# A two-layer hybrid diffusion step on one core: weight splits earlier, residual tiles in token halves, modulation rows moved

## The chip, the cores and the metric

One core of a Trainium2 chip runs the whole program in one launch. The metric is the device time of an execution in microseconds; the median of several runs is compared.

## What is computed

Two layers of a diffusion backbone over T = 640 tokens (128 of context, 512 latent ones), width 1024, all in float32. Each layer (from the reference, cut):

```python
mod = silu(cond) @ p['w_mod'][l] + p['b_mod'][l]
sh_a, sc_a, g_a, sh_f, sc_f, g_f = jnp.split(mod[:, None, :], 6, axis=-1)
xn = rmsnorm(h, p['norm_mix'][l]) * (1 + sc_a) + sh_a
proj = xn @ p['w_in'][l]
# three branches read proj: latent attention, gated linear attention, gated DeltaNet
y = jnp.sum(gates * proj_b, axis=2) @ p['w_out'][l]
h = h + g_a * y
xf = rmsnorm(h, p['norm_ffn'][l]) * (1 + sc_f) + sh_f
gu = xf @ p['ffn_w_in'][l]
h = h + g_f * ((silu(gu[..., :D_FF]) * gu[..., D_FF:]) @ p['ffn_w_out'][l])
```

A last rmsnorm gives the output, beside the caches and states of the branches. `cond` is one vector for the context tokens and one for the latent ones, so each row of `mod` has two columns.

## The kernel before

Activations stand channel by token: eight tiles of 128 channels by 640 tokens for h, and tokens are taken in two halves c = 0, 1 of HF = 320. Every float32 operand of a matmul is split in a high and a low part (xh, xl; wh, wl), and a product is three matmuls of 128x320: xh·wh, xl·wh, xh·wl. A weight block is 128 by up to 512, that is up to four k-steps of 128; an output tile with eight k-steps (wo, fg, fu, misc, mq) is 24 matmuls in each half, 48 in all.

Class `Stream` (L286) holds all such work of a layer as a list of units, one for a weight block or one product. `plain` (L312) adds one, `product` (L316) one of the seven block products of a gated pair, `step` (L341) issues one k-step, `to` runs until a tile is done, `fill` puts steps beside other work. `ahead` (L333) loads blocks and splits them: `wsplit` (L488) casts wr to wh on ACT (L493) and subtracts wl = wr - wh on POOL or DVE (L494). The ring of split blocks has three buffers. Accumulators are `gm` (three in PSUM). L539 (`mm_k`) is the matmul of plain units, L531 (`mm_block`) that of block products. A scheduler of the language then reorders the instructions of each engine by priority, keeping what depends on what; the order on an engine is fixed when the program is built.

A layer runs: norm and modulation (`modulate`, L677), input projections and the three branches, output tiles wo0 to wo7, the second norm (`modulate_in`, L696, and `token_sums`, L710, which makes the sums xeh, xel of token halves that block products need), then the FFN. Its 22 gate and up tile pairs (fg, fu) come in three groups of 8, 7 and 7. The first two pairs are plain tiles, the other 20 are seven block products of 12 matmuls each. A pair ends in th = silu(gate)·up, cast to ah (L1911) with al = th - ah (L1912). After each group its share of the second FFN matmul follows: tiles fo0_0 to fo0_7, then fo1, fo2, eight tiles each (42 or 48 matmuls); `h_update` (L725) adds gate times tile to h.

After wo7 and after fo2_7 comes a joint. `resid_posts` (L731) updates h tile by tile and `Norm.add` squares it (ACT, L659) and adds it to nacc (DVE, L660). The last tile is treated by halves (`Norm.end`). `Norm.fin` (L666) sums over partitions with a matmul by ones into `cs` (L669) and takes the reciprocal root as exp(-ln/2) on ACT (L551, L553), each with a table load in front. `join` (L746) orders this: half 0, then half 1, with the modulation of a half after its root. The tiles that follow (fg0 and fu0, or misc and mq0 of layer 1) need all eight modulated tiles, and no matmul that is left over stands beside that.

`ModVe` (L588) makes the rows of `mod` on DVE: one product with accumulation (L614) for each 128x512 piece of w_mod and each of the two conditions. They are called at chosen places (`some(...)`): beside wo tiles, in `close` of a pair, and in `fo_post` after a fo tile, and keep their order.

Of the kernel before, what the change touches and what calls it, by code (L numbers as in the profile page):

```python
# [18 lines left out]
P = 128  # L19
# [12 lines left out]
NPL = 2  # L32

# [254 lines left out]
class Stream:  # L288
# [44 lines left out]
    def ahead(self):  # L333
        u = self.units[self.u]
        i, c = u["i"], u["c"]
        self._split(i)
        top = max(self.w)
        for j in range(1, 3):
            self._load(top + j)
        if len(self.w) < self.ring and (top == i or (c == 1 and u["prod"] is None)):  # L340
            self._split(top + 1)  # L341

    def step(self):
# [14 lines left out]
        if self.k == kn:  # L358
# [5 lines left out]
            if u["prod"]:  # L364
# [36 lines left out]
def tile_hybrid(ctx: ExitStack, tc, a):  # L401
# [247 lines left out]
    class Norm:  # L649
        def __init__(self):  # L650
            self.acc = sp.tile([P, T], F32, name="nacc", tag="nacc", bufs=1)
            self.ps = self.last = None
# [8 lines left out]

        def end(self, h, c):
# [68 lines left out]
    def resid_posts(names, hs, g, nm, keep=False):  # L731
        def post(ps, c=None, d=0):
            if d < 7:
                h_update(hs, d, ps, g)
                nm.add(d, hs[d])
                if keep:
                    dma(hsp[d], hs[d])
            else:
                h_update(hs, d, ps, g, (c,))
                nm.end(hs[d], c)  # L740
                if keep:
                    dma(hsp[d][:, HS[c]], hs[d][:, HS[c]])
        for d in range(8):
            G.posts[names[d]] = lambda ps, c=None, d=d: post(ps, c, d)

    def join(name, hs, nm, after, pre=None):  # L746

        if pre:
            pre()
        G.to(name + "/0")  # L750
        G.steps(5)
        nm.fin(0)
        G.to(name)
        after(0, range(4))
        nm.fin(1)
        after(0, range(4, 8))
# [789 lines left out]

    for l in range(L):
# [485 lines left out]
```

## Time and profile before

| | |
|---|---|
| median of 3 runs | 2968.56 us (2960.3, 2970.24, 2968.56) |
| the profiled execution | 2961.4 us |
| its span, first to last instruction | 2959.3 us |
| mean granted clock of TensorE in it | 0.963 |
| busy: PE, DVE, ACT, POOL | 2691.0, 1888.7, 1390.0, 988.0 us |

The profiled execution is 7.2 us below the median and 2.1 above its own span. PE is TensorE, DVE VectorE, ACT ScalarE, POOL GpSimd. In a row, `a<-b,c` names what is written and read, L the line of the kernel; an idle time is that of the engine just before the instruction, with what ended it. A clock of 1.00 is 2.4 GHz, 0.50 is 1.2 GHz.

### The profile page before, as it was taken

To read this page: it belongs to the slowest core of one execution; us is meant where nothing else is said; L and a number is where in the kernel's file an instruction comes from. 1 tells how busy PE (TensorE), PEld (TensorE's weight loads), DVE (VectorE), ACT (ScalarE), POOL (GpSimd) and SP (SyncE) were. 2 spreads that over 40 slices of the span, in tenths; PEclk is the share of its full clock that TensorE was granted. 3 is DMA by queue.
4 is the path that set the end of the run, shared out by engine and by line. 5 is a ranking of instruction groups with operands and counts; after the bars stand their busy time and mean duration, and the time that the engine had idled before them with its cause. 6 is when DMAs were issued, how large, how long until landed. Compare 5 with 4: busy or idle time off the path is not lost. (4 is left out here: it accounts for less than half of the span.)

```text
span 2959.3 us, 50253 instructions
## 1 busy us (share of the span) xinstructions
PE 2691.0 (91%) x18964; PEld 2439.6 (82%) x18964; DVE 1888.7 (64%) x3712; ACT 1390.0 (47%) x2624; POOL 988.0 (33%) x748
## 2 busy tenths in 40 slices
PE   6899998899999789999988899988999997899998
PEld 4788887788879679898978888876878796899997
DVE  4766575657647687777458576566566466847374
ACT  5574646533333643434466555654333335424244
POOL 3443232333326313232335323233433352232313
PEclk9999999999999899999999999998999998999999
DMA  5254433255424234332223533332645151322222
GB/s 202 88 167 132 97 85 84 90 154 157 137 75 160 68 100 139 98 119 85 89 79 113 178 89 90 76 99 69 185 138 157 41 176 60 100 82 78 76 68 76
DMA packets 303601, 322.37 MB, mean 109 GB/s; under 512 B 164832, under 2 KB 175904, under 8 KB 303360
## 3 DMA queue, kind: packets, MB, share of 16 engines
q1 hardware_dynamic: 303360, 319.16, 36.4%
q8 instruction: 150, 2.46, 0.3%
q14 instruction: 91, 0.75, 0.1%
HBM read 271.25 MB, written 47.82 MB: 108 GB/s over the span
## 5 line engine op out<-in xcount | busy, mean ns | idle before, releaser
L494 POOL TENSOR_TENSOR wl<-wr,wh 128x512 fp32r<-128x512 f32 x496 | 691.7, 1398 | 1609.1 <-ACT wh L493 1371.5
L539 PE MATMUL gm<-xh,wh 128*128 128x320 f32 x2176 | 554.3, 330 | 39.1 <-ACT wh L493 11.5
L539 PE MATMUL gm<-xh,wl 128*128 128x320 f32 x2176 | 545.0, 323 | 19.9 <-POOL wl L494 19.9
L539 PE MATMUL gm<-xl,wh 128*128 128x320 f32 x2176 | 543.2, 323 | 11.3 <-DVE xl L707 3.8
L493 ACT ACTIVATE wh<-wr 128x512 fp32r<-128x512 f32 x496 | 305.5, 620 | 490.0 <-PE gm L539 231.5
L539 PEld LDWEIGHTS gm<-xh,wh 128*128 128x128 f32 x2176 | 378.5, 196 | 62.9 <-ACT wh L493 13.3
L539 PEld LDWEIGHTS gm<-xh,wl 128*128 128x128 f32 x2176 | 380.5, 195 | 32.2 <-POOL wl L494 23.7
L539 PEld LDWEIGHTS gm<-xl,wh 128*128 128x128 f32 x2176 | 381.5, 195 | 30.2 <-DVE xl L693 8.1
L614 DVE CUSTOM_DVE_ANT_0 ctb<-wmt,cbb 128x512 f32<-128x512 f32 x320 | 288.2, 901 | 2.8
L531 PE MATMUL gm<-xh,wh 128*128 128x320 f32 x640 | 203.9, 319 | 29.5 <-ACT wh L493 21.9
L531 PE MATMUL gm<-xh,wl 128*128 128x320 f32 x640 | 198.9, 311 | 3.3 <-POOL wl L494 3.3
L531 PE MATMUL gm<-xl,wh 128*128 128x320 f32 x640 | 198.8, 311 | 0.0
L493 ACT ACTIVATE wh<-ws 128x512 fp32r<-128x512 f32 x160 | 101.0, 632 | 175.9 <-PE gm L531 154.5
L531 PE MATMUL gm<-xeh,wh 128*128 128x320 f32 x480 | 152.8, 318 | 17.6 <-DVE su L1945 10.0
L539 PE MATMUL gm<-ah,wh 128*128 128x320 f32 x704 | 163.8, 310 | 3.9 <-ACT wh L493 3.7
L539 PE MATMUL gm<-al,wh 128*128 128x320 f32 x704 | 163.4, 308 | 0.0
L539 PE MATMUL gm<-ah,wl 128*128 128x320 f32 x704 | 162.5, 308 | 0.0
L531 PEld LDWEIGHTS gm<-xh,wh 128*128 128x128 f32 x640 | 121.4, 190 | 41.4 <-ACT wh L493 30.8
L1053 ACT ACTIVATE VN<-ch 64x64 f32<-64x64 f32 x320 | 70.0, 219 | 181.8 <-DVE vs L1050 160.3
L728 DVE SCALAR_TENSOR_TENSOR h<-gm,mod,h 128x128 f32<-128x128 f32 (+2 forms) x192 | 73.2, 432 | 118.8 <-PE gm L539 118.5
L531 PE MATMUL gm<-xel,wh 128*128 128x320 f32 x480 | 148.9, 310 | 0.0
L531 PE MATMUL gm<-xeh,wl 128*128 128x320 f32 x480 | 148.9, 310 | 0.0
(787 smaller groups left out, 5507.6 us busy)
## 6 DMA issues: line engine op xcount, KB each, us to landing
wr<-in_wall_dram SPq DMA_DIRECT2D x352, 256.0 KB, 2.7
wmt<-in_wmodt_dram SPq DMA_DIRECT2D x160, 256.0 KB, 3.0
wq<-in_wall_dram SPq DMA_DIRECT2D x80, 256.0 KB, 2.6
wr<-in_wfo_dram SPq DMA_DIRECT2D x64, 256.0 KB, 2.7
wr<-in_wbr_dram SPq DMA_DIRECT2D x48, 256.0 KB, 2.6
wm<-in_wmod_dram SPq DMA_DIRECT2D x16, 512.0 KB, 8.6
cbb<-in_condb_dram SPq DMA_DIRECT2D x14, 512.0 KB, 4.8
wr<-in_wfo_dram SPq DMA_DIRECT2D x32, 192.0 KB, 2.4
```

The costliest lines, as they stand in the source:

```text
L493: se.activation(wh[:, :w], wr[:, :w], AF.Copy)
L494: (ve if lo == "dve" else ge).tensor_tensor(wl[:, :w], wr[:, :w], wh[:, :w], op=ALU.subtract)
L531: pe.matmul(ps, w_[:, wsl], x_[k], start=(start and i == 0), stop=(stop and i == 2), skip_group_check=True)
L539: pe.matmul(ps[:, c, :HF], w_[:, wsl], x_[kx][:, c * HF:(c + 1) * HF], start=(start and i == 0), stop=(stop and i == 2))
L614: ins = ve.tensor_tensor_reduce(self.t, wm, self.c[:, i], 0.5, 0.0, ALU.mult, ALU.add, accum_out=acc[h][:, m - m0, i:i + 1])
L728: ve.scalar_tensor_tensor(hs[d][:, s:e], ps[:, c, s - c * HF:e - c * HF], g[:, d, i:i + 1], hs[d][:, s:e], op0=ALU.mult, op1=ALU.add)
L1053: se.activation(VN[d * 64:(d + 1) * 64, h, n], ps[h * 64:(h + 1) * 64, 1], AF.Copy)
```

## The change

1. `ahead` wants the blocks up to i + 2 split for products and half units, i + 1 for whole ones; before it was one ahead, with conditions.
2. The last three tiles of each residual sum (wo5 to wo7, fo2_5 to fo2_7) run by token halves: all three for half 0, then all three for half 1 (`by_halves`). Each half loads and splits its weights anew and has its own accumulator. The tiles that follow (fg0, fu0; misc, mq0 of layer 1) run by halves too. `Norm.part` squares a half; `Norm.fin` has an accumulator of its own. `join` runs one step of the second halves, the sum of half 0, then modulation tiles and steps in turn. The prescaling of us or h (`prescale`) goes by tile.
3. Rows 16 to 23 of layer 1's modulation are made in layer 0's FFN instead of the DeltaNet chain of layer 1. They are all called beside fo tiles, six products for a tile instead of three, and none in `close` for layer 1's rows. Beside wo: five products for each of wo0 to wo4 instead of four for wo0 to wo6.
4. al = th - ah runs on POOL instead of DVE.

```diff
@@ Stream
-        top = max(self.w)
         for j in range(1, 3):
-            self._load(top + j)
-        if len(self.w) < self.ring and (top == i or (c == 1 and u["prod"] is None)):
-            self._split(top + 1)
+            self._load(max(self.w) + j)
+        want = i + (1 if c is None else 2)
+        while len(self.w) < self.ring and max(self.w) < want and max(self.w) + 1 < len(self.subs):
+            self._split(max(self.w) + 1)
...
+            elif last and u["own"]:
+                with self.prio("pp"):
+                    self.posts.pop(name)(self.ps.pop(name)[:, :, :HF])
+                self.done.add(name)
@@ Norm, join
+        def part(self, h, c):
+            sq = tmp()
+            se.activation(sq[:, HS[c]], h[:, HS[c]], AF.Square)
+            ve.tensor_tensor(self.acc[:, HS[c]], self.acc[:, HS[c]], sq[:, HS[c]], op=ALU.add)
...
         def fin(self, c):
-            self.ps = psg("cs") if self.ps is None else self.ps
+            ps = psb([P, HF], "cs")
...
+    def join(name, l, nm, after):
+
+        G.to(f"{name}7.{l}:0")
+        G.steps(1)
         nm.fin(0)
-        G.to(name)
-        after(0, range(4))
+        for i in range(4):
+            after(0, range(2 * i, 2 * i + 2))
+            G.steps(2)
+        G.to(f"{name}7.{l}:1")
+        G.steps(1)
         nm.fin(1)
-        after(0, range(4, 8))
         after(1, range(8))
@@ the list of units
+    def by_halves(jobs, own):
+
+        for c in range(2):
+            for name, src, kt, xs in jobs:
+                for k0 in range(0, kt, 4):
+                    kn = min(4, kt - k0)
+                    G.plain(f"{name}:{c}" if own else name, src[:, k0 * P:(k0 + kn) * P], k0, kn, xs, c, k0 + kn == kt, False,
+                            own=own, key=f"{name}:{c}")
...
-            k8("misc", "in")
-            k8("mq0")
+            by_halves([w8("misc"), w8("mq0")], False)
...
-        for d in range(8):
-            k8(f"wo{d}", "post" if d == 7 else None)
+        for d in range(8 - NHV):
+            k8(f"wo{d}")
+        by_halves([w8(f"wo{d}") for d in range(8 - NHV, 8)], True)
...
-                k8(f"fg{f}", "in" if f == 0 else None)
-                k8(f"fu{f}", pre=lead and (lambda q=lead: q.fetch("A21", "A22")))
+                if f == 0:
+                    by_halves([w8("fg0"), w8("fu0")], False)
...
+            if tail:
+                by_halves([(f"fo{gi}_{d}.{l}", a["wfo"][l, d, :, f0 * P:f1 * P], f1 - f0, ("a",)) for d in range(8 - NHV, 8)], True)
@@ modulation rows and al
-                    mst = ModVe(bd, 4, 2).steps(l, range(16, 16 + OPT["mc"]))
+                    mst = ModVe(bd, 4, 2).steps(l, range(16 if l == 0 else NXT, 16 + OPT["mc"]))
...
-            nxt = mv.steps(l + 1, range(16), True) if l + 1 < L else iter(())
+            nxt = mv.steps(l + 1, range(NXT), True) if l + 1 < L else iter(())
...
-                ve.tensor_tensor(al[:, f - f0], th, ah[:, f - f0], op=ALU.subtract)
+                ge.tensor_tensor(al[:, f - f0], th, ah[:, f - f0], op=ALU.subtract)
...
-                elif f1 < NF:
-                    some(nxt, 2)
...
-                    some(nxt, 3 if (gi, d) != (gl_ - 1, 7) else 1000)
+                    some(nxt, 6)
```

Three places in the built order (NHV is 3, NXT is 24, a name with a number is one buffer).

**First place**: ACT at the start of the FFN of layer 0, before. L715 shifts us, L722 casts the token sums, wh_10324 is the weight block that L539 waits for.

```order
L722 ACTIVATE xeh_10048<-tsum_10238 128x960 [waits DVE_49]
L715 ACTIVATE us7_10061<-us7_10061,mod0_102 128x128
L722 ACTIVATE xeh_10048<-tsum_10249 128x960 [waits DVE_49]
L715 ACTIVATE us7_10061<-us7_10061,mod0_102 128x512 [waits Activation_49]
L493 ACTIVATE wh_10324<-wr_10279 128x512 [waits DMAHW3_49,PE_49]
L493 ACTIVATE wh_10370<-wr_10310 128x512 [waits DMAHW4_49,PE_49]
L1905 ACTIVATE th_10340<-gm_10281 128x640 [waits PE_49]
L722 ACTIVATE xeh_10048<-tsum_10260 128x960 [waits DVE_49]
```

The same place in the change: L727 and L734 are the lines of the shifts and casts now, and wh_10386 is the second block of fg0 in half 1.

```order
L734 ACTIVATE xeh_9926<-tsum_10286 128x960 [waits DVE_49]
L727 ACTIVATE us6_9544<-us6_9544,mod0_102 128x128
L727 ACTIVATE us6_9544<-us6_9544,mod0_102 128x512 [waits Activation_49]
L727 ACTIVATE us3_9541<-us3_9541,mod0_102 128x128
L727 ACTIVATE us3_9541<-us3_9541,mod0_102 128x512
L734 ACTIVATE xeh_9926<-tsum_10297 128x960 [waits DVE_49]
L727 ACTIVATE us7_9545<-us7_9545,mod0_102 128x128
L734 ACTIVATE xeh_9926<-tsum_10308 128x960 [waits DVE_49]
L727 ACTIVATE us7_9545<-us7_9545,mod0_102 128x512 [waits Activation_49]
L500 ACTIVATE wh_10386<-wr_10365 128x512 [waits DMAHW3_49,PE_49]
L500 ACTIVATE wh_10404<-wr_10384 128x512 [waits DMAHW4_49,PE_49]
L500 ACTIVATE wh_10422<-wr_10402 128x512 [waits DMAHW5_49,PE_49,Pool_49]
```

The cast of the weight block stands behind the shifts and casts of the token sums in both; in the change it is the block of fg0's second half, and two more blocks stand next to it.

**Second place**: PE at the end of wo7 of layer 0, before. gm_10082 is wo7, cs the sum over partitions for both halves.

```order
L669 MATMUL cs_10138<-th_10115,ones_79 128x320 [waits Activation_49]
L539 MATMUL gm_10082<-xh_98,wh_10078 128x320
L539 MATMUL gm_10082<-xl_99,wh_10078 128x320
L539 MATMUL gm_10082<-xh_98,wl_10079 128x320
L539 MATMUL gm_10082<-xh_98,wh_10078 128x320
L539 MATMUL gm_10082<-xl_99,wh_10078 128x320
L539 MATMUL gm_10082<-xh_98,wl_10079 128x320
L539 MATMUL gm_10082<-xh_98,wh_10078 128x320
L539 MATMUL gm_10082<-xl_99,wh_10078 128x320
L539 MATMUL gm_10082<-xh_98,wl_10079 128x320
L669 MATMUL cs_10138<-nacc_9530,ones_79 128x320 [waits Activation_49]
L669 MATMUL cs_10138<-th_10115,ones_79 128x320 [waits Activation_49]
```

In the change, gm_10080 is the second half of wo5, and cs_10084 the sum for half 0 alone.

```order
L546 MATMUL gm_10080<-xh_98,wh_10035 128x320 [waits DVE_49,Activation_49]
L546 MATMUL gm_10080<-xl_99,wh_10035 128x320
L546 MATMUL gm_10080<-xh_98,wl_10036 128x320 [waits Pool_49]
L681 MATMUL cs_10084<-nacc_9531,ones_79 128x320 [waits DVE_49]
L546 MATMUL gm_10080<-xh_98,wh_10035 128x320
L546 MATMUL gm_10080<-xl_99,wh_10035 128x320
L546 MATMUL gm_10080<-xh_98,wl_10036 128x320
L546 MATMUL gm_10080<-xh_98,wh_10035 128x320
L546 MATMUL gm_10080<-xl_99,wh_10035 128x320
L546 MATMUL gm_10080<-xh_98,wl_10036 128x320
L546 MATMUL gm_10080<-xh_98,wh_10035 128x320
L681 MATMUL cs_10084<-th_10072,ones_79 128x320 [waits Activation_49]
```

The sum of half 0 stood among the matmuls of wo7's second half, next to that of half 1; now it stands at the head of the second half of wo5, with nearly three half tiles of matmuls behind it.

**Third place**: DVE in a pair of group 0 of layer 0, before. ISA is a modulation product (L614), su (L1945) a sum that the next block product's accumulator waits for.

```order
L1953 TENSOR_TENSOR th<-th,su 128x320
L1912 TENSOR_TENSOR al<-th,ah 128x640
L614 ISA ctb,mod_102<-wmt,cbb 128x512
L614 ISA mod_102 128x1
L494 TENSOR_TENSOR wl<-wq,wh 128x512
L614 ISA ctb,mod_102<-wmt,cbb 128x512
L614 ISA mod_102 128x1
L614 ISA ctb,mod_102<-wmt,cbb 128x512
L614 ISA mod_102 128x1
L1945 TENSOR_TENSOR su<-gm,sn 128x320
L614 ISA ctb,mod_102<-wmt,cbb 128x512
L614 ISA mod_102 128x1
```

In the change (L621, L1983; the subtraction that makes al is on POOL):

```order
L1991 TENSOR_TENSOR th<-th,su 128x320
L621 ISA ctb,mod_102<-wmt,cbb 128x512
L621 ISA mod_102 128x1
L621 ISA ctb,mod_102<-wmt,cbb 128x512
L621 ISA mod_102 128x1
L621 ISA ctb,mod_102<-wmt,cbb 128x512
L621 ISA mod_102 128x1
L501 TENSOR_TENSOR wl<-wq,wh 128x512
L621 ISA ctb,mod_102<-wmt,cbb 128x512
L621 ISA mod_102 128x1
L1983 TENSOR_TENSOR su<-gm,sn 128x320
```

al is gone from this engine; three products stand in a row ahead of wl, and su stands behind all four instead of three.

## Rows read from the trace of the kernel before

**Rows 1.** The page, parts 1 and 2: PE, and the clock by slices.
```profile
PE 2691.0 (91%) x18964; PEld 2439.6 (82%) x18964; DVE 1888.7 (64%) x3712; ACT 1390.0 (47%) x2624; POOL 988.0 (33%) x748
PEclk9999999999999899999999999998999998999999
```

**Rows 2.** Windows: stretch, us; busy (x) of PE, PEld, DVE, ACT, POOL; clock, DMA, GB/s.
```profile
951.80:1022.40 70.60, 49.99 (x243) 44.03 (x243) 49.34 (x100) 44.95 (x86) 23.21 (x17) 0.81 0.23 71
1463.60:1515.10 51.50, 40.82 (x221) 36.15 (x220) 29.89 (x53) 30.68 (x58) 18.03 (x16) 0.87 0.22 72
2416.60:2487.20 70.60, 51.63 (x250) 46.33 (x249) 49.48 (x100) 44.93 (x86) 23.22 (x17) 0.78 0.23 72
1140.00:1260.00 120.00, 114.35 (x760) 111.08 (x759) 96.21 (x183) 43.11 (x76) 34.35 (x24) 1.00 0.40 125
2600.00:2720.00 120.00, 115.27 (x765) 112.02 (x765) 68.71 (x118) 42.29 (x74) 32.18 (x25) 1.00 0.26 79
```

**Rows 3.** Timeline of PE, first joint: start, us, line, tiles, [idle <-releaser].
```profile
979.28 1.41 PE L669 MATMUL cs<-nacc,ones 128*128 128x320 f32 x2 [4.76 <-DVE nacc L660]
989.55 0.81 PE L669 MATMUL cs<-th,ones 128*128 128x320 f32 x2 [2.22 <-ACT th L664]
1015.02 0.56 PE L539 MATMUL gm<-xh,wh 128*128 128x320 f32 x2 [3.96 <-ACT wh L493]
1017.74 0.90 PE L539 MATMUL gm<-xh,wl 128*128 128x320 f32 x2 [1.87 <-POOL wl L494]
```

**Rows 4.** Timeline of PE in group 1: two matmuls at either clock.
```profile
1258.66 0.31 PE L531 MATMUL gm<-xh,wh 128*128 128x320 f32 x1
1258.81 0.31 PE L531 MATMUL gm<-xl,wh 128*128 128x320 f32 x1
1265.57 0.47 PE L531 MATMUL gm<-xl,wh 128*128 128x320 f32 x1
1265.83 0.47 PE L531 MATMUL gm<-xh,wh 128*128 128x320 f32 x1
```

**Rows 5.** Lines of ACT, 980 to 1016 us: busy, mean ns of one, idle before.
```profile
L705 ACT ACTIVATE xh<-us,mod 128x128 fp32r<-128x128 f32 (+2 forms) x24 | 9.4, 460 | 2.2 <-DVE us L700 1.3 <-POOL us L700 0.9
L715 ACT ACTIVATE us<-us,mod 128x128 f32<-128x128 f32 (+1 forms) x16 | 7.8, 548 | 0.0
L722 ACT ACTIVATE xeh<-tsum 128x960 fp32r<-128x960 f32 x3 | 3.0, 1000 | 0.0
```

**Rows 6.** Timeline of PE, second joint.
```profile
1487.45 0.81 PE L669 MATMUL cs<-nacc,ones 128*128 128x320 f32 x2 [2.22 <-ACT nacc L551]
1491.90 0.90 PE L539 MATMUL gm<-xh,wh 128*128 128x320 f32 x2 [3.11 <-ACT xh L686]
```

**Rows 7.** The page, part 5, and one wait of a pair in PE's timeline.
```profile
L531 PE MATMUL gm<-xh,wh 128*128 128x320 f32 x640 | 203.9, 319 | 29.5 <-ACT wh L493 21.9
...
1398.67 0.42 PE L531 MATMUL gm<-xh,wh 128*128 128x320 f32 x1 [0.62 <-ACT wh L493]
```

**Rows 8.** Timeline of DVE and POOL at the end of group 1.
```profile
1294.81 0.82 DVE L1912 TENSOR_TENSOR al<-th,ah 128x640 fp32r<-128x640 f32 x1 [0.81 <-ACT ah L1911]
1295.55 1.78 DVE L614 CUSTOM_DVE_ANT_0 ctb<-wmt,cbb 128x512 f32<-128x512 f32 x1
1297.37 0.69 DVE L614 CUSTOM_DVE_ANT_0 ctb<-wmt,cbb 128x512 f32<-128x512 f32 x1
1297.99 1.13 DVE L728 SCALAR_TENSOR_TENSOR h<-gm,mod,h 128x128 f32<-128x128 f32 x3
...
1295.38 1.40 POOL L494 TENSOR_TENSOR wl<-wr,wh 128x512 fp32r<-128x512 f32 x1 [2.98 <-ACT wh L493]
```

**Rows 9.** Timeline of ACT after the last matmul: the root of the second half.
```profile
2948.60 0.53 ACT L551 ACTIVATE nacc<-cs,epsD 128x320 f32<-128x320 f32 x1
2949.14 1.28 ACT L553 ACT_TABLE_LOAD   x1
2950.44 0.47 ACT L553 ACTIVATE nacc<-nacc 128x320 f32<-128x320 f32 x1
```

More of the change, by code (lines that the diff above doesn't have):

```diff
@@ L32 @@
 NPL = 2
+NHV = 3
+NXT = 24
 O_MQ, O_CKV, O_KR = 0, 256, 384
@@ L651, in __init__ @@
             self.acc = sp.tile([P, T], F32, name="nacc", tag="nacc", bufs=1)
-            self.ps = self.last = None
+            self.last = None
         def add(self, d, h):
@@ L1545, in job, with w8 @@
                 pre = None
+    def by_halves(jobs, own):
+        for c in range(2):
+            for name, src, kt, xs in jobs:
[3 more added lines that the diff above has]
+                            own=own, key=f"{name}:{c}")
     for l in range(L):
+        def w8(n, l=l):
+            return f"{n}.{l}", a["wall"][l, TILES[n]], 8, xs8
         def k8(n, halves=None, ks=None, l=l, pre=None):
@@ L1618, in tile_hybrid @@
             fo(1, [(4, kf - 4)])
-            for d in range(2, 8):
-                n = pairs[f1] if d == 7 and gi + 1 < len(GROUPS) else None
+            tail = gi + 1 == len(GROUPS)
+            for d in range(2, 8 - NHV if tail else 8):
+                n = pairs[f1] if d == 7 else None
                 fo(d, pre=n and (lambda n=n: n.fetch("A21", "A22")))
+            if tail:
+                by_halves([(f"fo{gi}_{d}.{l}", a["wfo"][l, d, :, f0 * P:f1 * P], f1 - f0, ("a",)) for d in range(8 - NHV, 8)], True)
     def fill(name):
@@ L1861, in tile_hybrid @@
         nm = Norm()
-        resid_posts([f"wo{d}.{l}" for d in range(8)], hs, mod[:, 16:24], nm)
+        upctx = [pool("xe", "left"), pool("us", "left")]
+        xep, up = [c_.__enter__() for c_ in upctx]
+        us = [up.tile([P, T], F32, name=f"us{d}") for d in range(8)]
+        resid_posts("wo", l, hs, mod[:, 16:24], nm,
+                    halved=lambda d, c: prescale(us, hs, mod[:, 32:40], range(d, min(d + 1, 7)), c))
         def some(steps, n):
@@ L1868, in tile_hybrid @@
         mvs = mv.steps(l, range(16 + OPT["mc"], 40), True)
-        for d in range(7):
+        for d in range(8 - NHV):
             G.to(f"wo{d}.{l}")
-            some(mvs, 4)
+            some(mvs, 5)
         some(mvs, 1000)
@@ L1885, in tile_hybrid @@
             cur["X"][f"T{j + 2}"] = tuple([x[:, k, j] for k in range(4)] for x in (xeh, xel))
-        with pool("us", "left") as up:
-            us = [up.tile([P, T], F32, name=f"us{d}") for d in range(8)]
-            join(f"wo7.{l}", hs, nm, lambda c, ds: modulate_in(hs, us, nm.acc, mod[:, 32:40], mod[:, 24:32], c, ds),
-                 lambda: prescale(us, hs, mod[:, 32:40]))
-            token_sums(us, mod[:, 24:32], xeh, xel, xt1, up)
+        prescale(us, hs, mod[:, 32:40], range(8 - NHV))
+        join("wo", l, nm, lambda c, ds: modulate_in(hs, us, nm.acc, mod[:, 32:40], mod[:, 24:32], c, ds))
+        token_sums(us, mod[:, 24:32], xeh, xel, xt1, up)
+        upctx[1].__exit__(None, None, None)
         with pool("fp", "left") as fp, pool("sw", "left") as sw, pool("sn", "left") as sn:
@@ L1978, in tile_hybrid @@
             nm = Norm()
-            resid_posts([f"fo{gl_}_{d}.{l}" for d in range(8)], hs, mod[:, 40:48], nm, l + 1 < L)
-            G.to(f"fo{gl_}_6.{l}")
             if l + 1 < L:
+                sc_n = mods[l + 1][:, 8:16]
+            else:
+                sc_n = fn.unsqueeze(2).to_broadcast([P, 8, 2])
+            resid_posts(f"fo{gl_}_", l, hs, mod[:, 40:48], nm, l + 1 < L,
+                        lambda d, c: prescale(hs, hs, sc_n, range(d, min(d + 1, 7)), c))
+            if l + 1 < L:
+                G.to(f"fo{gl_ - 1}_7.{l}")
+                some(nxt, 1000)
                 for s_ in range(2):
@@ L1999, in result @@
                         dma(a["yt"][d][:, HS[c]], t[:, HS[c]])
-                def scaled():
-                    for d in range(7):
-                        se.activation(hs[d], hs[d], AF.Copy, scale=fn[:, d:d + 1])
-                join(f"fo{gl_}_7.{l}", hs, nm, result, scaled)
-        xctx.__exit__(None, None, None)
+                G.to(f"fo{gl_}_{7 - NHV}.{l}")
+                prescale(hs, hs, sc_n, range(8 - NHV))
+                join(f"fo{gl_}_", l, nm, result)
+        upctx[0].__exit__(None, None, None)
         mvctx.__exit__(None, None, None)
```

62 lines of the change are left out of this document (33 added, 29 removed).

## The prediction

> **What bounds the kernel now.** The page first: PE is busy for 91% of the span, the other engines for 64% at most, and the granted clock is below full speed in a few slices only [rows 1]. So what can be won is PE time that is not spent on matmuls at full pace, and the question is where it lies. The table by windows answers that [rows 2]. In the middle of a gated FFN PE is busy for 115 of 120 us at a clock of 1.00. Around the places where a sum over all eight tiles of h must be known before the next matmul can start (I call them joints), it is busy for 50 of 70.6 us at 0.81, 41 of 51.5 at 0.87 and 52 of 70.6 at 0.78. The first and third window run from the last matmul of wo4 to the last of fu0 (layers 0 and 1), the second from the end of fo2_4 to the end of mq0. A fourth joint is the end of the program.
>
> What a window would take without loss: a 128x320 matmul starts 0.147 us after the one before at 2.4 GHz, and 0.267 us at 1.2 GHz, which is what rows show after a wait [rows 4]. The first joint holds five tiles of 48 matmuls, 240 x 0.1465 = 35.2 us, and four f32 sums over partitions (cs), some 2.8 us: 38.0. So 32.6 us are lost there, and the same in the third. The second holds three tiles of 42 (6.15 us each) and two of 48 (7.03), with the sums 33.7 us; 17.8 are lost. 83 us in three places are the prize.
>
> The timeline of PE shows how they go [rows 3]: 4.76 us until DVE has added the last square to nacc, 2.22 until the second half's square, and later 3.96 and 1.87 for the parts wh and wl of one weight block. After each the matmuls run at the lower clock for some time. In the second joint it is the reciprocal root (2.22) and then the first xh (3.11) [rows 6]. The 3.96 has its cause on ACT: the weight's cast stands behind the token sums, whose rows L715 and L722 fill ACT just before it [rows 5].
>
> **The change part by part.**
>
> *Splits two blocks ahead.* The pair stage is where this could count: there the row of L531 waits 21.9 us for wh over the whole run [rows 7]. A single wait of the pattern is 0.62 us, once a pair: PE's order places two matmuls of the next pair in front of a product that still reads the third buffer, so the cast can start only when PE has passed the earlier product. The ring stays at three. The built order of PE and ACT in a pair is the same before and after, waits too; the scheduler had moved the splits up already. I cost it at 0; between 0 and the whole 21.9.
>
> *Joints by halves, first and third.* Six half blocks (wo5 to wo7) instead of three tiles: the first halves end 10.6 us after wo4 (3 x 3.52), the second ones some 10.6 after that, so the sum, root and modulation of half 0 have that long. DVE's update of h7 and ACT's square come first (in the second place of the order PE reaches cs after three matmuls of wo5's second half). I put the second cs at 14.2: DVE has two products and four modulation rows ahead of it. Then the root: two table loads of 1.28, Ln 0.53 and Exp 0.47, 3.6 us [rows 9], with a weight cast between them 18.4. The first xh are there before PE has ended the second halves, which weight splits behind the table loads stretch to about 25. So the wait of 4.76 and most of the 2.22 go. What is late next is half 1: cs about 29, root 33.4, fg0's second half from 35, its first block done at 37.8. Its second block needs a cast that now stands on ACT behind 8 xh of half 1, 12 shifts of us and 3 casts of xeh (the first place of the order): 8 x about 0.55 (the 24 of the row, mostly smaller pieces, average 0.460), 12 x 0.548 and 3 x 1.000 make 14 us [rows 5], some 15 with the waits for DVE between, and the cast itself is done at about 49. PE stands for 11 us there, where before it stood 3.96. Three blocks of 12 follow at 0.267 (3.2 us each) with a wl of 1.3 or so ahead of each: the end is at 58.6 instead of 70.6. That is 12.0; I take **-11.5** for each of the two, with 0 (the ACT chain decides alone) and -32.6 (all cover holds) as ends. It is nearer to the small end because the one wait that grows is on the path.
>
> *Second joint.* No token sums here. Half 0 of fo2_7 ends at 9.2 us; sum and root take until 16.5, PE has the second halves until 18.5. The modulated tiles then come at about 1 us each where PE needs 0.44 for one of 12 matmuls, so misc and mq0 end half 0 at 27; half 1's cs stands within mq0's first half, its root ends at 30, xh at 31, and the tiles come again at 1 us: 40.7 instead of 51.5. **-10**, between 0 and -17.8.
>
> *The end.* The tail after the last matmul holds one root instead of a part of both: one load of 1.28 less, at most two [rows 9]. **-1.5**, between 0 and -4.
>
> *36 more weight blocks* (24 of wall, 12 of wfo) are loaded and split anew: an SP transfer, a cast on ACT and some 1.4 us of POOL [rows 8] each. In the wo stage they lie beside 3.52 us of matmuls per block pair; hidden, 0. Where ACT has a table load in front, it is in the walk above.
>
> *Modulation rows.* 32 products leave the DeltaNet chain of layer 1, where PE is busy all the time: 0. Seven pairs of group 1 lose two each; that stretch has 0.9 us less of PE than its like in layer 1 without such products [rows 2]: **-1**. The fo tiles get six each instead of three. A tile is 6.2 to 7.0 us long; DVE needs 1.13 for h and six of 0.69 to 0.9 [rows 8], at most 6.5. It fits, barely; h would wait up to 5 us for its turn, which three accumulators cover.
>
> *al on POOL.* DVE gives up 44 x 0.82 us, POOL takes 44 of about 1.6 (estimate: the wl row of 512 columns scaled to 640) [rows 8]. In a pair, al and wl now follow each other on POOL while DVE has its products (the third place of the order): such a product took 0.69 us alone and 1.78 beside wl, so being beside POOL costs 1.1. It matters where su comes behind four products, in group 0, some 12 pairs: between 0 and 12 x 1.1 = 13, I take **+3**, nearer the small end as su's row then waits only for what is left. The last al of a group has about 4 us until fo reads it: 0. The Trainium skill's page "Perfetto Trace Analysis", section "Optimizing Scalar/DVE Operations", speaks against this move: as GPSIMD and DVE share an SBUF read port, shifting work between these two might not help. By it the +3 would be nearer to +13; the row of 1.78 agrees with the sharing.
>
> Sum: -23 - 10 - 1.5 - 1 + 3 = **-32.5**. The profiled execution would go from 2961.4 to 2929. The median of the three runs is 7.2 above that execution, so I state the time on the median's scale: 2968.6 - 32.5 = 2936.
>
> **The rivals.**
> (a) *The splits ahead do take away the ring's wait.* Then some 22 us more go: 2914. For it: the rows name wh. Against: the same order, the same ring. 0.06.
> (b) *The joints are covered almost entirely*, because half 1's chain runs beside half 0's matmuls and ACT does not hold the cast for 11 us: 0.75 of 83 us, some -62: 2907. For it: the work is there to hide it. Against: the 23 operations in front of the cast. 0.14.
> (c) *Slower: POOL's al holds DVE in every pair.* 40 pairs; if su or th is late by 1.1 us in each, and PE loses another 0.5 at the lower clock after it, 64 us against 35.5 won: 2997. It decides from 0.9 us a pair. For it: 1.78 beside 0.69, and DVE's 64%. Against: su and th read PSUM, DVE has 0.82 less per pair, and a wait of 0.62 a pair leaves the clock at 1.00. 0.07. The page "SBUF — State Buffer" of the Trainium skill, section "SBUF: two separate sides", calls the port a lock that one engine holds for its whole instruction, which would be this case.
> (d) *Won and given back*: the cast behind the token sums stops PE longer than it stopped it before, the lower clock follows, and the joints come out even. 2966, no change. 0.10.
>
> **How the numbers follow.** The forecast (joints worth 15 to 50 in all) has 0.63. Two executions of this kernel differ by up to 0.3%, about 9 us, so that is what can be told from no change. Faster: 0.63 + 0.06 + 0.14 = 0.83; same 0.10; slower 0.07. The range goes from (b), 2907 less some scatter, to (d), 2966; (c) is left out.
>
> **What would show it.** Right: the windows of the three joints shorter by about 12, 10 and 12 us; no wait of cs for nacc above 1 us; a wait of fg0's second half for a wh of about 11 us, ACT full before it; a pair as long as now, with its 0.62; customs of DVE in group 0 longer. Wrong: a pair shorter by half a us (a), longer by one (c), or a first joint as long as it was (d).

## The result and the profile after

| | before | after |
|---|---|---|
| median of 4 runs each, same chip | 2969.40 us (2960.30 to 2970.76) | 3008.99 us (3006.35 to 3013.55) |
| the profiled execution, its span | 2961.4, 2959.3 us | 3013.55, 3011.5 us |

The ratio is 1.0142 (95% interval 1.0118 to 1.0165): slower by 40 us, where 32 us less was forecast. The time lies outside the stated range, above it.

Page of the kernel after, part 1:
```profile
PE 2708.4 (90%) x18964; PEld 2455.9 (82%) x18964; DVE 1905.9 (63%) x3676; ACT 1418.8 (47%) x2685; POOL 1110.0 (37%) x828
```

Against [rows 1] the shares hardly move, and PE has as many matmuls as before, 18964. That allows the best reading of where the time went: take the n-th matmul in both traces and subtract its start. The lead or lag of the kernel after at places of the program follows (time in the trace of before, then lag). The times are bounds of the windows (those of [rows 2] among them) and lie within 2 us of the named end; the lag at the end itself is the same within 0.2.

| place | before, us | after minus before, us |
|---|---|---|
| end of wo4, layer 0 | 951.8 | -1.1 |
| end of fu0 (first joint) | 1022.4 | -1.4 |
| end of the pairs of group 0 | 1137.3 | +7.9 |
| fo0 done, group 1 begun | 1210.0 | +23.6 |
| last pairs of group 1 | 1294.0 | +22.5 |
| fo1 done, group 2 begun | 1360.0 | +29.4 |
| end of fo2_4 | 1463.6 | +29.9 |
| end of mq0 (second joint) | 1515.1 | +27.5 |
| end of wo4, layer 1 | 2416.6 | +41.2 |
| end of fu0, layer 1 (third joint) | 2487.2 | +42.8 |
| end of the pairs of group 0, layer 1 | 2602.0 | +52.0 |

Of the +52 between these two executions, 9 are group 0 of layer 0, 16 are fo0, 7 are fo1 and 9 group 0 of layer 1: 41 in four stretches, about what the medians differ by. Of the 14 that appear between 1515 and 2417, 3.3 come right behind mq0 (by 1600), and 2.5 to 4.2 in every kernel with the halves, so the second joint gives back what it won. The other 10 lie in the branches of layer 1 and differ from run to run: two kernels below that are as before there (`before_tsums` and `before_al_pool`) show 0.5 and 9.4 in their profiled executions. The three joints give -0.3, -2.4 and +1.6: nothing.

The windows of after, the first and second joint, the pairs of group 0, and fo0 with the start of group 1; columns as in [rows 2]:
```profile
950.70:1021.00 70.30, 46.62 (x242) 41.33 (x242) 50.74 (x93) 51.87 (x100) 36.81 (x27) 0.81 0.32 98
1493.50:1542.60 49.10, 38.37 (x220) 33.87 (x220) 32.15 (x52) 33.94 (x68) 31.11 (x25) 0.97 0.41 123
1022.50:1145.10 122.60, 104.83 (x644) 100.66 (x644) 89.74 (x144) 47.64 (x83) 38.64 (x25) 0.93 0.31 96
1145.10:1235.00 89.90, 74.38 (x479) 72.03 (x478) 78.25 (x168) 21.07 (x37) 27.54 (x18) 0.92 0.48 154
```

The last two stretches in the kernel before:
```profile
1024.00:1137.30 113.30, 99.84 (x645) 95.77 (x644) 85.37 (x150) 47.35 (x83) 24.98 (x18) 0.98 0.32 101
1137.30:1210.00 72.70, 69.90 (x469) 68.56 (x468) 56.98 (x112) 20.05 (x35) 24.55 (x17) 1.00 0.42 133
```

The first joint is 70.3 us long where it was 70.6 [rows 2]. The pairs of group 0 take 9.3 more at a lower clock. fo0 takes 17.2 more, and there DVE is busy for 78 of 90 us.

The waits of PE, whole run, after and then before (us in total, times, longest):
```profile
PE gm L538 <- DVE th L1977: 25.1, 6, 11.2
PE gm L538 <- ACT wh L500: 20.3, 34, 0.6
PE gm L538 <- DVE su L1983: 19.2, 9, 2.4
```
```profile
PE gm L531 <- DVE su L1945: 10.0, 13, 1.9
PE gm L531 <- DVE th L1939: 7.4, 6, 2.4
```

Two waits of the block products for DVE have grown, by 9.2 and 17.7 us; the wait for wh is what it was [rows 7]. The largest single one stands behind fo0, in the timeline of PE:
```profile
1211.21 0.64 PE L538 MATMUL gm<-xeh,wh 128*128 128x320 f32 x1 [11.22 <-DVE th L1977]
1211.64 0.47 PE L538 MATMUL gm<-xel,wh 128*128 128x320 f32 x1
1211.90 0.47 PE L538 MATMUL gm<-xeh,wl 128*128 128x320 f32 x1
```

What DVE did in that stretch, out of the lines of 1145.1 to 1235 (busy, mean ns | idle before), with the same lines of 1137.3 to 1210 in the kernel before:
```profile
L621 DVE CUSTOM_DVE_ANT_0 ctb<-wmt,cbb 128x512 f32<-128x512 f32 x56 | 50.1, 895 | 1.1
L740 DVE SCALAR_TENSOR_TENSOR h<-gm,mod,h 128x128 f32<-128x128 f32 (+2 forms) x24 | 9.5, 432 | 0.1
```
```profile
L614 DVE CUSTOM_DVE_ANT_0 ctb<-wmt,cbb 128x512 f32<-128x512 f32 x28 | 28.5, 1019 | 0.6
L728 DVE SCALAR_TENSOR_TENSOR h<-gm,mod,h 128x128 f32<-128x128 f32 (+2 forms) x24 | 9.0, 430 | 0.8 <-PE gm L539 0.7
```

56 modulation products in place of 28 are 21.6 us more of DVE, in a stretch in which it had 15.7 left (72.7 less 56.98). PE's next pair waits for a `th` that stands at the end of that queue; its first matmuls after the wait start 0.26 us apart, the lower clock of [rows 4].

### The profile page after: what moved, and what is told of

Same layout as the page of the kernel before. It is cut to its first block, busy times and chain, and to the rows that moved or that the text cites. A ratio compares the mean times of both kernels' runs of the same rounds, so it can differ in the third digit from the quotient of the medians.

```text
span 3011.5 us, 50567 instructions
## 1 busy us (share of the span) xinstructions
PE 2708.4 (90%) x18964; PEld 2455.9 (82%) x18964; DVE 1905.9 (63%) x3676; ACT 1418.8 (47%) x2685; POOL 1110.0 (37%) x828
## 5 line engine op out<-in xcount | busy, mean ns | idle before, releaser
L501 POOL TENSOR_TENSOR wl<-wr,wh 128x512 fp32r<-128x512 f32 (+1 forms) x532 | 741.9, 1398 | 1463.1 <-ACT wh L500 1229.1
L546 PE MATMUL gm<-xh,wh 128*128 128x320 f32 x2176 | 563.8, 329 | 42.5 <-ACT wh L500 26.3
L546 PE MATMUL gm<-xh,wl 128*128 128x320 f32 x2176 | 554.6, 324 | 23.2 <-POOL wl L501 22.9
L500 ACT ACTIVATE wh<-wr 128x512 fp32r<-128x512 f32 (+1 forms) x532 | 327.1, 619 | 514.4 <-PE gm L546 218.3
L546 PE MATMUL gm<-xl,wh 128*128 128x320 f32 x2176 | 551.3, 323 | 12.9 <-DVE xl L705 5.3
L546 PEld LDWEIGHTS gm<-xh,wl 128*128 128x128 f32 x2176 | 382.4, 195 | 39.3 <-POOL wl L501 29.9
L621 DVE CUSTOM_DVE_ANT_0 ctb<-wmt,cbb 128x512 f32<-128x512 f32 x320 | 291.1, 910 | 9.1 <-DMA wmt<-in_wmodt_dram 5.1
L538 PE MATMUL gm<-xh,wh 128*128 128x320 f32 x640 | 204.4, 320 | 26.6 <-ACT wh L500 20.3
L538 PE MATMUL gm<-xh,wl 128*128 128x320 f32 x640 | 198.8, 311 | 4.1 <-POOL wl L501 4.1
L538 PE MATMUL gm<-xeh,wh 128*128 128x320 f32 x480 | 159.1, 331 | 44.7 <-DVE th L1977 25.1
L538 PE MATMUL gm<-xl,wh 128*128 128x320 f32 x640 | 199.1, 311 | 0.0
L538 PEld LDWEIGHTS gm<-xeh,wh 128*128 128x128 f32 x480 | 95.1, 198 | 55.6 <-DVE su L1983 28.9
```

What stands on the lines that cost most here:

```text
L500: se.activation(wh[:, :w], wr[:, :w], AF.Copy)
L501: (ve if lo == "dve" else ge).tensor_tensor(wl[:, :w], wr[:, :w], wh[:, :w], op=ALU.subtract)
L538: pe.matmul(ps, w_[:, wsl], x_[k], start=(start and i == 0), stop=(stop and i == 2), skip_group_check=True)
L546: pe.matmul(ps[:, c, :HF], w_[:, wsl], x_[kx][:, c * HF:(c + 1) * HF], start=(start and i == 0), stop=(stop and i == 2))
L621: ins = ve.tensor_tensor_reduce(self.t, wm, self.c[:, i], 0.5, 0.0, ALU.mult, ALU.add, accum_out=acc[h][:, m - m0, i:i + 1])
```

## The experiments

"Rows" below are the modulation rows. Twelve kernels ran, in three groups of four, and the kernel before ran beside each group. Its medians there were 2965.6, 2966.7 and 2967.3 us, and 2969.4 beside the kernel after; so a difference in us between kernels of two groups holds within some 4 us, and the ratios to the kernel before are the safer measure.

**1. Undo one part at a time.** `al_dve` is the change with al back on DVE:
```diff
-                ge.tensor_tensor(al[:, f - f0], th, ah[:, f - f0], op=ALU.subtract)
+                ve.tensor_tensor(al[:, f - f0], th, ah[:, f - f0], op=ALU.subtract)
```


> The change with al made on DVE again; all else stays. Theory R (six modulation products for each fo tile overload DVE; al does little): the pairs of group 0 lose su's wait of 1.7 to 2.4 us at most, so 3009 goes to 2995 to 3009, and the wait of 11.2 us for th at the start of group 1 stays. Theory A (al on POOL holds DVE's operations wherever POOL works): the two groups 0, which take 122.6 and 122.8 us here against 113.3 and 113.5 before, go back by 9 each, and the fo tiles gain too: 2985 or below.

Measured: 2990.61 us (2982.12 to 2993.92), 1.0082 (1.0061 to 1.0103); 18.4 below the kernel after. It lies between the two theories: by the lag of matmuls the two groups 0 come back by 12 us each (theory A has 9), and fo0 still loses 17 (theory R).

`rows_back` has NXT = 16, three products per fo tile and two in `close`, as before:
```diff
-NXT = 24
+NXT = 16
...
-                    some(nxt, 6)
+                    some(nxt, 3 if (gi, d) != (gl_ - 1, 7) else 1000)
...
+                elif f1 < NF:
+                    some(nxt, 2)
```


> The change with the modulation rows of layer 1 divided as before: 16 columns in layer 0's FFN, three products for a fo tile and two in a pair of group 1, 20 columns in the DeltaNet chain; al stays on POOL. Theory R: the waits for th at the start of groups 1 and 2 go (11.2 us the longest), the stretch of fo0 with the start of group 1 goes from 89.9 back to about 73 us, that of fo1 from 73.0 to 66: about 2987. Theory A: the two stretches stay over 80 and 70 us, 3000 or more.

Measured: 2987.84 us (2986.89 to 2994.55), 1.0084 (1.0065 to 1.0104); 21.2 below, or 17 by the ratios; theory R's number. In the lag of matmuls, the stretch of fo0 comes back by 16 us and that of fo1 by 6.

`joints_ahead` has both edits, so of the change only the joints, the splits and the five products for a wo tile are left.

> The change with both undone, al on DVE and the rows divided as before: what is left are the joints by halves and the splits ahead. If the two parts add up and the joints earn nothing: 2969, equal to before. If the joints earn what was forecast: 2935. If the joints by themselves cost, above 2975.

Measured: 2967.41 us (2960.48 to 2971.37, 10 runs), 1.0002 (0.9993 to 1.0012). The two costs add up within the noise (18.4 and 21.2 alone, 41.6 together), and what was to bring 33 us brings none.

`ahead_back` is the change with the old rule of `ahead`.

> The change with the earlier rule for splitting ahead; joints by halves, rows and al as in the change. The order in the pairs is the same, so the pairs do not move. Where the halves run, a block's cast is called one block later: 3009 within 5 if the scheduler evens that out, 3015 to 3025 if the half blocks need it.

Measured: 3011.33 us (3007.17 to 3016.78), 1.0157 (1.0139 to 1.0176), within 3 us of the kernel after. The splits ahead are worth nothing, as the prediction costed them; rival (a) falls.

**2. Why al on POOL costs 18 us.** A pair of group 0 in the timeline of DVE, after:
```profile
1113.81 1.06 DVE L1991 TENSOR_TENSOR th<-th,su 128x320 f32<-128x320 f32 x1
1114.80 0.68 DVE L621 CUSTOM_DVE_ANT_0 ctb<-wmt,cbb 128x512 f32<-128x512 f32 x1
...
1116.25 1.96 DVE L621 CUSTOM_DVE_ANT_0 ctb<-wmt,cbb 128x512 f32<-128x512 f32 x1
...
1118.15 1.75 DVE L501 TENSOR_TENSOR wl<-wq,wh 128x512 fp32r<-128x512 f32 x1
1119.82 0.68 DVE L621 CUSTOM_DVE_ANT_0 ctb<-wmt,cbb 128x512 f32<-128x512 f32 x1
...
1120.43 0.48 DVE L1983 TENSOR_TENSOR su<-gm,sn 128x320 f32<-128x320 f32 x1
```
POOL and PE in it:
```profile
1115.73 1.94 POOL L1952 TENSOR_TENSOR al<-th,ah 128x640 fp32r<-128x640 f32 x1 [1.20 <-ACT ah L1951]
1117.83 1.52 POOL L501 TENSOR_TENSOR wl<-wr,wh 128x512 fp32r<-128x512 f32 x1 [0.16 <-ACT wh L500]
```
```profile
1120.96 0.55 PE L538 MATMUL gm<-xeh,wh 128*128 128x320 f32 x1 [2.38 <-DVE su L1983]
```
The same pair with al on DVE, DVE and then PE:
```profile
1103.83 1.06 DVE L1991 TENSOR_TENSOR th<-th,su 128x320 f32<-128x320 f32 x1
1105.69 0.83 DVE L1952 TENSOR_TENSOR al<-th,ah 128x640 fp32r<-128x640 f32 x1 [0.80 <-ACT ah L1951]
...
1108.38 0.48 DVE L1983 TENSOR_TENSOR su<-gm,sn 128x320 f32<-128x320 f32 x1
```
```profile
1108.92 0.41 PE L538 MATMUL gm<-xeh,wh 128*128 128x320 f32 x1 [0.32 <-DVE su L1983]
```

su starts 6.6 us after th in the one and 4.6 in the other. Two things differ: without al on DVE the scheduler placed four products and wl ahead of su in place of two and wl, and two of DVE's operations take 1.75 to 1.96 us, in place of 0.68, beside those of POOL. Theory Place says that it is the position, theory Port that it is POOL. `own_after_su` keeps al on POOL and calls the four products behind su, pinned there (six pairs of each group 0):
```diff
-                    some(own, 4 if f + 1 < f1 else 1000)
+                    some(own, (4 if f < NPL else 0) if f + 1 < f1 else 1000)
...
-                        ve.tensor_tensor(u, ps[:, 1, :HF], s_[3], op=ALU.add)
+                        ins = ve.tensor_tensor(u, ps[:, 1, :HF], s_[3], op=ALU.add)
                         g.append(u)
+                        if f0 == 0:
+                            tc.keep_in_program_order(ins)
+                            some(own, 4)
```


> The change, al on POOL as in it, but the four modulation products of a pair of group 0 are called after su and kept behind it. The loss of al on POOL was 18 us, all in the two groups 0. Theory Place (su is late because it stands behind four products where it stood behind two or three): the groups 0 go from 122.6 back to 113 or 114 us each, so 2990. Theory Port (POOL's al and wl hold DVE's products and wl beside them, wherever su stands): DVE is late at other places of the pair, th or wl, and the groups stay above 118 us: 3000 or more.

Measured: 2989.33 us (2987.4 to 2991.8), 1.0081 (1.0063 to 1.0099), 19.7 below the kernel after with al still on POOL, as theory Place has it. It is level with `al_dve`, but not place by place: it is 1.2 and 3.4 us behind that kernel in the two groups 0 and 5.4 ahead in fo0, so some cost of al on POOL stays in the pairs.

`before_al_pool` is the kernel before with al on POOL and nothing else.

> The kernel before with al on POOL and nothing else. If the loss is that of this part alone: 2966 + 18 = 2984, su waits of 1.7 to 2.4 us in the groups 0. If it needs the rest of the change (half blocks, more products for a fo tile): within 5 of 2966.

Measured: 2986.32 us, 1.0069 (1.0052 to 1.0086): this one line costs 20 us in the kernel before too. Its matmuls fall back by 7 us in group 0 of either layer, and in groups 1 and 2 by 0; the other 6 us were not located.

**3. Why the joints bring nothing.** PE in the first joint of the kernel after: its waits of 1.1 us and more, and the two matmuls at 981, the last of wo7's second half and the first of fg0:
```profile
953.93 0.41 PE L546 MATMUL gm<-xh,wl 128*128 128x320 f32 x1 [1.35 <-POOL wl L501]
956.96 0.41 PE L546 MATMUL gm<-xh,wh 128*128 128x320 f32 x1 [1.30 <-ACT wh L500]
...
969.70 0.81 PE L681 MATMUL cs<-th,ones 128*128 128x320 f32 x2 [1.95 <-ACT th L676]
...
981.22 0.31 PE L546 MATMUL gm<-xh,wl 128*128 128x320 f32 x1
981.46 0.41 PE L546 MATMUL gm<-xh,wh 128*128 128x320 f32 x1
...
989.54 1.44 PE L681 MATMUL cs<-nacc,ones 128*128 128x320 f32 x2 [1.70 <-DVE nacc L672]
999.99 0.42 PE L546 MATMUL gm<-xl,wh 128*128 128x320 f32 x1 [2.27 <-DVE xl L719]
1011.74 0.63 PE L546 MATMUL gm<-xh,wh 128*128 128x320 f32 x1 [9.64 <-ACT wh L500]
1014.45 0.64 PE L546 MATMUL gm<-xh,wl 128*128 128x320 f32 x1 [1.81 <-POOL wl L501]
```
ACT just before the 9.64 ends:
```profile
1005.27 1.00 ACT L734 ACTIVATE xeh<-tsum 128x960 fp32r<-128x960 f32 x1
1006.18 1.90 ACT L727 ACTIVATE us<-us,mod 128x128 f32<-128x128 f32 x4
...
1011.08 1.65 ACT L500 ACTIVATE wh<-wr 128x512 fp32r<-128x512 f32 x3
```
The wait of 4.76 of [rows 3] is down to 1.70, and one of 9.64 stands in place of 3.96: the cast of fg0's second block (in half 1) stands behind the token sums, which the block products need only after fu0 and two more plain tiles (fg1, fu1). Theory Cast says that this wait is real lost time; its rival, that something behind it would take its place. `tsums_late100` is `joints_ahead` with a later priority for the token sums; `before_tsums` is the kernel before with that alone:
```diff
-        token_sums(us, mod[:, 24:32], xeh, xel, xt1, up)
+        with defer(100):
+            token_sums(us, mod[:, 24:32], xeh, xel, xt1, up)
```


> The joints by halves and splits ahead (al and rows as before), with the token sums given a later priority, so that the casts of fg0's and fu0's second halves stand ahead of most of them on ACT. Theory Cast (the waits of 9.1 and 1.8 us for wh and wl after the sums take what the halves win): 5 to 9 us less in each of the first and third joint, 2949 to 2957. Theory Chain (half 1's own chain, cs at 995 and its last xh at 1009, sets the end whatever the cast does): 0 to 3 us less in each, 2961 to 2967.

Measured: 2953.57 us (2950.99 to 2957.65), 0.9961 (0.9947 to 0.9974): 13.8 below `joints_ahead`, and **faster than both kernels** (0.4% below before). That is theory Cast's number. Of the table's places, the end of fu0 of layer 0 is at -9.8 (in `joints_ahead` +3.6); by the end of group 0 it is -2.4 (+0.6), so most of that is given back there. The end of the second group 0 is at -3.1 (+5.0).

> The kernel before with the token sums at the same later priority and nothing else. The waits of 3.96 and 1.87 us after them go, twice, and some of the lower clock behind them: 2966 - 10 = 2956 by theory Cast; 2966 within 3 if the time goes into a later wait for xeh or for th.

Measured: 2963.29 us (2955.02 to 2966.22), 0.9983 (0.997 to 0.9995), 3.4 below before. So by the medians and ratios the halves alone are worth nothing, the late sums alone 3 to 5 us, and both together 12 to 13. The last two intervals touch, and the traces do not show the two parts helping one another. By the lag of matmuls, from the end of wo4 to the end of the group 0 behind it, `joints_ahead` gains 3.4 and 0.5 us in the two layers, `before_tsums` 4.7 and 3.0, and both together 4.0 and 7.5, 11.5 in all against 11.6 for the sum of the two. The halves then lose 3 us again behind the last group (from 2900 on). The profiled execution of `tsums_late100` is 4.1 us above its median and that of `before_tsums` 8.3 below, so where the 9.7 us between the two medians lie stays open.

**4. What can be had beside that.** The first is `best_dve`: `tsums_late100` with the products of group 0 behind su. The other three start from it.

> The joints by halves and the splits ahead, with the modulation rows as before, al on VectorE, the token sums at a later priority and, in group 0, the four own products called behind su and pinned behind it. Theory Place (in group 0 what hurts is work that VectorE does ahead of su): with al on VectorE and the products as before, su still ended one wait in the trace of that kernel, in most pairs under 0.4 us; so 8 pairs by up to 0.4 us in two layers, at most 6 us below the kernel with the sums late alone (2953.6): 2948 to 2953, ratio 0.994 to 0.996. Rival (the products behind su make the last product, and so fo0, late): 2954 to 2958.

Measured: 2954.84 us (2953.14 to 2960.39), 0.9967 (0.9954 to 0.9979), the same as `tsums_late100` and in the rival's range: with al on DVE, pinning su ahead of the products brings nothing.

> As best_dve, but al on GpSimd. Theory Place: GpSimd's al stands in no path once su goes ahead of the products; within 2 us of best_dve. Rival Port (VectorE's products and GpSimd's al slow one another, three products a pair at 1.7 to 2 us in place of 0.7, and the extra 3 us of VectorE a pair make su late by themselves): 10 to 20 us more than best_dve, 2960 to 2970.

Measured: 2963.31 us (2959.33 to 2970.21, 11 runs), 0.9991 (0.998 to 1.0003), 8.5 above `best_dve`; as a time it is in rival Port's range, as a difference just under its 10. By the lag of matmuls `best_pool` loses 5.6 on `best_dve` from fu0 to the end of fo0 in layer 0, and 2.7 in group 0 of layer 1. The lines of DVE from 1030 to 1145, `best_dve` and then `best_pool`:
```profile
L628 DVE CUSTOM_DVE_ANT_0 ctb<-wmt,cbb 128x512 f32<-128x512 f32 x34 | 28.4, 836 | 0.3
L508 DVE TENSOR_TENSOR wl<-wq,wh 128x512 fp32r<-128x512 f32 x6 | 4.1, 687 | 4.4 <-ACT wh L507 4.4
```
```profile
L628 DVE CUSTOM_DVE_ANT_0 ctb<-wmt,cbb 128x512 f32<-128x512 f32 x33 | 30.5, 925 | 0.3
L508 DVE TENSOR_TENSOR wl<-wq,wh 128x512 fp32r<-128x512 f32 x6 | 8.9, 1481 | 12.2 <-ACT wh L507 12.2
```
The wl of DVE ahead of su takes 1.48 us on the mean with al on POOL, in place of 0.69. So position is the larger part of al's cost, and a smaller one stays when position is mended. The longer wl and products say that this part comes from being beside POOL; no run took that apart from the new order of DVE.

> As best_dve, with eight modulation products per tile of wo in place of five, so that the rows which the next root needs are done sooner. Theory A (at joints 1 and 3 ScalarE's scaling of the halves waits 3.1 us for the modulation's rows, ahead of the first high halves, and TensorE's 1.35, 1.30 and 0.80 us of idle there come from it): 3 us less per joint, 6 in all, 2942 to 2948. Rival B (those 3.5 us are given back in the wait for the cast behind them, or eight per tile hold the eviction of wo): within 2 us of best_dve, or up to 8 slower.

Measured: 2960.98 us (2955.96 to 2964.35, 11 runs), 0.9978 (0.9968 to 0.9988), by its median 6.1 above `best_dve`, within rival B's range; the intervals overlap. ACT's wait for the rows, in the kernel after and in this one:
```profile
955.08 1.31 ACT L687 ACTIVATE us<-h,mod 128x128 f32<-128x128 f32 x3 [3.11 <-DVE mod L636]
```
```profile
959.13 2.22 ACT L694 ACTIVATE us<-h,mod 128x128 f32<-128x128 f32 x5 [1.76 <-DVE mod L643]
```
It is shorter, PE's 1.35 is down to 0.28, and its 1.30 and 0.80 stay (1.28, 0.79); but the wait of 1.95 for the last square has become 3.24. That is not theory A's 6 us, and this wait is not what holds the joint.

> As best_dve, with the rows of the change, 24 per block, but four per tile of the second product in place of six, and two in each pair of groups 1 and 2 as before. Theory Rate (VectorE was full at six per tile, 48 products and h at 65 us; at four it has 16 products of 0.7 us less, 11 us of slack): within 4 us of best_dve. Rival (any further product beside fo costs its time, since h for the next group waits behind them): 16 products a block fewer in the pairs give nothing, and 0 to 8 us a layer more; 2953 to 2970.

Measured: 2970.36 us (2962.71 to 2978.47, 12 runs), 1.0012 (1.0002 to 1.0021), 15.5 above `best_dve` and just above the rival's range. fo0 at four per tile costs nothing (the lag grows by 3.0 across it, in `best_dve` by 2.5), and the pairs of group 1, which keep their products, gain 3.0. But fo1 loses 9.7: from 1285 to 1357 DVE has 46 products and is busy for 62.5 of 72 us (`best_dve`: 28, and 49.4 of 66), and the next pair waits 7.5 us for th, as after fo0 in the kernel after. Theory Rate falls as stated: four a tile are hidden in one fo stretch, and not in the other, where more land.

## Why the prediction was wrong, by its own steps

**Two terms costed near 0 are the slowdown.** *Six products per fo tile* was "It fits, barely", 0. It cost 21.2 us (`rows_back`; 17 by the ratios), 16 in fo0 and 6 in fo1. The step compared only h and six products with the time of a tile. Its price of a product, 0.69 to 0.9, was low already: the 28 products of that stretch take 1.019 on the mean in the kernel before, so six and h are 7.2 us, not 6.5, against a tile of 6.2 to 7.0. And DVE had other work there: it was busy for 57 of 72.7 us, by a window of before that the prediction does not show, and 24 more products of 0.9 us (three for each of eight tiles) exceed the 15.7 that were free. The three accumulators do cover h; but the first block products of the next group wait for DVE as well, in order behind all of that.

*al on POOL* was +3, and cost 18 to 20. Its upper end was 13, from 1.1 us for one product beside POOL in 12 pairs. (Its 1.6 for al was low too: 1.40 for 512 columns scaled to 640 is 1.75, and the pair shown took 1.94.) The order of DVE that stood ahead of the prediction showed su behind four products instead of three. The step priced the length of one product and not the place of su: up to 2.38 us of wait in a pair, in a stretch at a clock of 0.93. Rival (c) had the engine and the sign, but in every pair; pairs without own products cost nothing (-1.1 and +0.5 in groups 1 and 2 of layer 0, in the table above). The port that the Trainium skill's page "SBUF — State Buffer", section "SBUF: two separate sides", calls a lock would be what is left in `best_pool`, 8.5 us of the 20; products of 0.68 and 1.96 us in one pair agree with it. The Trainium skill's page "Perfetto Trace Analysis", section "Optimizing Scalar/DVE Operations", had warned that such a move might not help, as the two engines share a read port. The runs bear out the warning; but its reason, the two engines side by side, is by `best_pool` the smaller part of the loss.

**The joints, -33, brought 0.** The walk of the first joint against the trace, from the start of its window (950.7, the end of wo4 within half a us):

| step | predicted, us | measured, us |
|---|---|---|
| last matmul of the first halves | 10.6 | 15.1 |
| sum of half 0 | 14.2 | 19.0 |
| last matmul of the second halves | 25 | 30.8 |
| sum of half 1 | 29 | 40.1 |
| its root | 33.4 | 44 |
| wait for the cast | 11 | 9.64 |
| end of fu0 | 58.6 | 70.9 |

The cast behind the token sums was foreseen, and nearly its size. What failed is the line before it, "cs about 29": the sum of half 1 comes 11.1 us later than walked, in three parts. The first halves lose 4.5, of which 3.6 are waits for weight parts (1.35, 1.30, 0.80, 0.17), where the walk took 3.52 for a half tile, no wait at all. The tiles wo5 to wo7 of the kernel before already wait 3.8 for weights, of which the largest is
```profile
965.08 0.56 PE L539 MATMUL gm<-xh,wh 128*128 128x320 f32 x2 [1.56 <-ACT wh L493]
```
The second halves take 15.7 where 14.4 were walked; 13 of their matmuls start 0.27 us apart after the wait of 1.95, the others 0.15. The largest part, 5.3, lies behind them: from the last matmul of wo7's second half to the sum of half 1 the walk has 4 us and the trace 9.3. DVE in that time, out of its timeline:
```profile
974.32 3.38 DVE L712 TENSOR_TENSOR us<-us,nacc 128x320 f32<-128x320 f32 x3
...
980.02 3.19 DVE L719 SCALAR_TENSOR_TENSOR xl<-us,mod,xh 128x192 fp32r<-128x192 f32 x7
...
986.92 0.54 DVE L740 SCALAR_TENSOR_TENSOR h<-gm,mod,h 128x320 f32<-128x320 f32 x1
...
988.55 0.54 DVE L740 SCALAR_TENSOR_TENSOR h<-gm,mod,h 128x320 f32<-128x320 f32 x1
989.01 0.47 DVE L672 TENSOR_TENSOR nacc<-nacc,th 128x320 f32<-128x320 f32 x1
```
PE is done with the second halves of wo6 and wo7 at 977.6 and 981.5, but h for them is made at 986.9 and 988.6: DVE has the modulation of half 0 (us, xl) in front, and the square, nacc and the sum of half 1 follow h. So the work that was to be hidden beside the second halves is itself what holds half 1. The order is the same in `joints_ahead`, `tsums_late100` and `best_dve`, and no run changed it, so what it would bring is not shown.

Behind the wait for the cast the walk also adds up wrongly: from 49, three blocks of 3.2 give 58.6 without the wl of 1.3 ahead of each that it names; with them the end is 62.5, and the gain 8.1 instead of 12.0. The trace has one such wait, 1.81.

*36 more weight blocks* at 0 is not refuted. The waits of plain matmuls in the whole run, after and then before, are
```profile
PE gm L546 <- ACT wh L500: 30.1, 15, 9.8
PE gm L546 <- POOL wl L501: 24.4, 25, 4.5
```
```profile
PE gm L539 <- POOL wl L494: 19.9, 14, 4.8
PE gm L539 <- ACT wh L493: 15.3, 11, 4.1
```
Of the 14.8 more for wh, 11.4 are the cast behind the token sums in the first and third joint (9.64 and 9.8 in place of 3.96 and 4.10).

From the sum of half 1 on, everything is 11 to 12 us late. So the joint came out even, as in rival (d). Its cause, the longer wait for the cast, is there too, but the forecast had counted that wait; what it had not counted stands in front of it.

*The second joint*, -10, measured -2.4. The second halves end at 23.0 where 18.5 was walked, misc and mq0 of half 0 at 36.5 where 27 was, and after the sums of half 1 PE waits 2.50 and 1.39. *The end*, -1.5, measured +0.3 (lag +51.9 at 2900, +52.2 at the end of the span): the second halves lose 3.4 by the last matmul (+55.3), and the shorter tail wins 3.1 back, within the -4 allowed for it.

*Right*: the splits ahead, 0; the 32 products out of the DeltaNet chain, no gain seen. *Right by number alone*: group 1, -1 without its products, -1.1 in the table. Kernels that keep those products gain as much there (-1.1 in `before_al_pool`, -2.0 in `rows_back`), so it is not theirs.

Faster had 0.83 because every joint counted as won, and the two costs that could turn the sign were priced by one operation each.

Open: why the branches of layer 1 take up to 11 us more in some executions, and what the joints bring when DVE makes h of half 1 ahead of the modulation of half 0.

## What to carry to other kernels

Before work is moved beside a stage, take that stage's own window of the receiving engine: busy time, plus what is added, against its length; a per-tile balance of two operations leaves out what else stands there. When an operation leaves an engine whose order a scheduler builds, look for the one instruction that the bottleneck waits for, and count what now stands ahead of it; if it matters, pin it. And before a joint is halved, look at what each engine has in its queue between the two halves: here the modulation of half 0 stood on DVE in front of h of half 1, and the token sums on ACT in front of a weight's cast. The halves were worth 0 alone, and 12 to 13 us together with the token sums moved back, of which those alone give 3 to 5; the traces do not show that the two help one another.

## What was not expected of the hardware

A DVE product of 128x512 took 0.68 us with POOL idle and 1.96 beside a POOL subtraction of 128x640, and the DVE wl in front of su 1.48 on the mean with al on POOL (`best_pool`), 0.69 without (`best_dve`). In the kernel before, a product beside POOL's wl took 1.78 [rows 8] and the longest of all 1.91. And in the pairs of group 0 of layer 0, PE waits four times for su in both kernels, 4.3 us in all before and 8.8 after, with longest waits of 1.9 and 2.38; the granted clock of the stretch is 0.98 before and 0.93 after, while waits like the 0.62 of [rows 7], once a pair, leave the windows of [rows 2] in the FFN at 1.00.
